# Summing the squares of six RMS norms with a block of ones, in a hybrid decoder step on one core

## The chip, the core and the metric

The kernel runs on one core of a Trainium2 chip. A core has a matrix engine (TensorE, PE in the profile; the loads of its stationary operand stand there as PEld), a vector engine (VectorE, DVE), an activation engine (ScalarE, ACT), a general engine (GpSimd, POOL) and a queue engine that issues the DMAs (SyncE, SP). [...] The metric is the device time of one execution in microseconds (us), as a median over runs.

## The reference, cut to what matters

One decoder layer over 304 tokens (16 meta, 256 prompt, 8 sequences of 4 sample tokens). Every RMS norm divides a token's row by the root of its mean square:

```python
def rmsnorm(x, g):
    xf = x.astype(jnp.float32)
    y = xf * lax.rsqrt(jnp.mean(xf * xf, axis=-1, keepdims=True) + EPS)
    return (y * g.astype(jnp.float32)).astype(x.dtype)

# layer, for prompt and sample tokens
proj = rmsnorm(x, g_mix) @ w_in
lru_out = rmsnorm(hl * gelu(gate_lru), g_lru_out)            # over 2048 features
yg = yg * lax.rsqrt(mean(yg * yg, axis=-1) + EPS)            # SSD: 4 groups of 512 features
x = x + concat([lru_out, yg * g_ssd_out]) @ w_out
x = x + square(relu(rmsnorm(x, g_mlp) @ w_up)) @ w_down
y = rmsnorm(x, g_final)
```

That makes eight norms: one on the input, four on the SSD groups, one on the RG-LRU output, one before the MLP and the last one.

## The kernel before

**Layout.** Features lie on the 128 partitions, tokens on the columns (T = 304 columns, or NT = 288 without the meta tokens). A row of 2048 features is 16 such tiles. The sum over features of one token is therefore a sum over partitions, which only TensorE does here.

**Matrix products.** Weights come from HBM as blocks of 128 output features (1 MB each). `prep` loads a block into one of two buffers `wraw`; ACT copies it, rounded, to `whi`, and DVE subtracts to get `wlo`, in two halves (four buffers of each). The activations are split in the same way into a high and a low part. `gemm` makes 16 x 3 matmuls per block (line 101) into one PSUM bank of a pool of three (`g`); the first three blocks take banks of another pool of five (`s`), from which `bank()` serves all small products too. What follows a block (`post`: read the bank, convolve, gate, square) runs on ACT, DVE and POOL beside the next blocks.

**Order.** Small jobs are Python generators. `pump` advances the first one in the list `gens` at four places in each block, so a `yield` moves what follows it about a quarter of a block (some 12 matmuls) down. A scheduler then lays out each engine's list from the dependences; copies of weights have priority.

**The stages.** (1) Input: the first 13 blocks multiply the x that is not yet normalized (`x0`), and their results are scaled by 1/rms (`rsb`); until `rsb` is there, the posts are kept in the list `held`. `norm_x` makes `rsb`, releases the held posts, and then makes the normalized operands `xa` (line 241 scales, ACT copies `xh`, DVE subtracts `xl`), which the later blocks use. (2) Blocks for the SSD inputs, with the SSD cores of four groups between them; `h` are state tiles, loaded by DMA and split by ACT (`h0h`) and POOL (`h0l`). (3) Blocks for the gates z; `norm_z(g)` norms one group. (4) RG-LRU blocks (`post_gate`, `post_xl`, `gates`). (5) Output projection: 16 blocks on the SSD part, in whose first blocks `norm_lru` runs, and 16 on the LRU part. (6) MLP: four rounds of 16 blocks up and 16 down. (7) The final norm and the store.

**The norm itself.** ACT, DVE or POOL square the tiles and add them up to one tile of 128 partitions. `ms_add` (line 161) then takes this tile as stationary operand, 128 tokens at a time, and a column of ones as moving operand: three products of one column, which put the tokens on the partitions. `rs_from` (lines 163 to 167) takes root and reciprocal of that 128 x 3 tile on ACT and DVE. Two yields later `rs_bcast` (line 169) spreads the result over all partitions again, by three products with the identity (line 172). `norm_x` and `norm_lru` then copy it from PSUM to SBUF on ACT; `norm_z` has DVE read it from PSUM. The norm before the MLP (`norm_x1`) and the last one use `ms_add` and `rs_bcast` too.

Of the kernel before, what the change touches and what calls it, by code (L numbers as in the profile page):

```python
# [8 lines left out]
F32 = mybir.dt.float32  # L9
F32R = mybir.dt.float32r  # L10
AF = mybir.ActivationFunctionType
# [3 lines left out]
P = 128  # L15
T = 304          # 16 meta, 256 prompt, 8 x 4 sample tokens
M0 = 16          # first token whose output is needed
NT = 288         # tokens with an output
FL = 328         # columns of the flat convolution
EXT = 331        # 3 zeros, 272 prompt columns, 8 x (3 old + 4 new) sample columns  # L20
S0 = 275         # first sample column of the flat layout
EPS = 1e-6
NK = 16          # 128-row tiles of a 2048-long contraction

# columns of the per-feature parameters
# [3 lines left out]
# columns of the constants  # L29
# [4 lines left out]
def body(ctx, tc, I, O):  # L34
# [12 lines left out]
    def nm(s):  # L47
        cnt[0] += 1
        return f"{s}_{cnt[0]}"
# [13 lines left out]
    def act(out, in_, f, bias=None, scale=None):  # L63
        kw = {}
        if bias is not None:
            kw["bias"] = bias
        if scale is not None:
            kw["scale"] = scale
        A.activation(out, in_, f, **kw)  # L69
# [3 lines left out]
    # ---------------------------------------------------------------- weights  # L73
# [33 lines left out]
    # blocks: (weights, operands, first column, last column, what follows)  # L107
# [35 lines left out]
    # ---------------------------------------------------------------- constants  # L143
# [14 lines left out]
    # ---------------------------------------------------------------- RMS norm  # L158
# [3 lines left out]

    def rs_from(ms, n):
        r3 = cst.tile([P, 3], F32, tag="r3", bufs=2, name=nm("r3"))
        act(r3[:], ms[:, 0:3], AF.Sqrt, bias=epst[:], scale=1.0 / n)
        V.reciprocal(r3[:], r3[:])
        return r3
# [8 lines left out]
    # ---------------------------------------------------------------- start  # L176
    # The first blocks take x as it comes and their results are scaled by 1 / rms; the
    # normalized x of the later blocks is made meanwhile.
# [40 lines left out]
    def norm_x():  # L219
        for k in range(8, NK):  # L220
            sq = sp.tile([P, EXT], F32, tag="th", bufs=2, name=nm("sq"))
            act(sq[:, :T], xts[k][:], AF.Square)
            tt(V, sqa, sqa, sq[:, :T], ADD)
        for _ in range(7):
            yield
        ms = bank()
        ms_add(ms, sqa, T, True, True)
        r3 = rs_from(ms, 2048.0)
        yield
        yield  # L230
        bc = rs_bcast(r3, T)
        act(rsb[:], bc[:, :T], AF.Copy)
        for b in held:
            b()
        held.clear()
        scaled.append(True)
        yield
        for k in range(NK):
            hi = a1p.tile([P, T], F32R, tag="ah", name=nm("xh"))
            lo = a1p.tile([P, T], F32R, tag="al", name=nm("xl"))  # L240
            tc.keep_in_program_order(V.scalar_tensor_tensor(
                xts[k][:], xts[k][:], par[:, C_GMIX + k:C_GMIX + k + 1], rsb[:], op0=MUL, op1=MUL))
            act(hi[:], xts[k][:], AF.Copy)
            tt(V, lo[:], xts[k][:], hi[:].bitcast(F32), SUB)
            xa.append((hi, lo))
            yield
            yield
            yield
# [3 lines left out]
    # ---------------------------------------------------------------- other resident data  # L252
# [9 lines left out]
    hw = cst.tile([P, 152], F32, name="hw")      # halves of conv_ssd_w, conv_ssd_b; lru_ba, lru_bx  # L262
# [42 lines left out]
    # ---------------------------------------------------------------- SSD: B, C, x  # L305
# [84 lines left out]
    # ---------------------------------------------------------------- SSD core of one group  # L390
# [6 lines left out]
    # Tokens of a chunk on the partitions; "sm" has the 32 sample tokens three times and then the  # L397
    # 16 meta tokens, so that one pass sums the products of high and low parts.
    def ssd_core(g):
# [5 lines left out]
        # C of each sequence in columns of its own, high and low parts  # L405
# [84 lines left out]
        # states: after the meta tokens, after chunk 1, after chunk 2  # L490
        hst = [sq_.tile([P, 512], F32, tag="hst", bufs=3, name=nm("hst")) for _ in range(3)]
        yield
        # decay between the tokens of a chunk, for each head
# [109 lines left out]
    # ---------------------------------------------------------------- input projection, SSD part  # L603
# [33 lines left out]
    def norm_z(g):  # L637
        yield
        yield
        ms = bank()  # L640
        ms_add(ms, yg_sq[g], NT, True, True)
        r3 = rs_from(ms, 512.0)
        yield
        yield
        bc = rs_bcast(r3, NT)
        for i in range(4 * g, 4 * g + 4):
            yy = yt_[i][:, :NT]
            stt(yy, yy, par[:, C_GSSD + i:C_GSSD + i + 1], bc[:, :NT], MUL, MUL)
            if i % 2:
                yield  # L650
# [30 lines left out]
    # ---------------------------------------------------------------- second operand set  # L681
# [14 lines left out]
    # ---------------------------------------------------------------- RG-LRU  # L696
# [80 lines left out]
    # With w = tanh(-log(a) / 2): 1 - a^2 = w (1 + a)^2.  # L777
# [43 lines left out]
    # ---------------------------------------------------------------- output projection  # L821
# [3 lines left out]
    def norm_lru():  # L825
        yield
        yield
        ms = bank()
        ms_add(ms, lsq, NT, True, True)
        r3 = rs_from(ms, 2048.0)  # L830
        yield
        yield
        bc = rs_bcast(r3, NT)
        rs = lp.tile([P, NT], F32, tag="sq", bufs=2, name="rsl")
        act(rs[:], bc[:, :NT], AF.Copy)
        for h in range(16):
            hi = a1p.tile([P, T], F32R, tag="ah", name=nm("lh"))
            lo = a1p.tile([P, T], F32R, tag="al", name=nm("ll"))
            u = us[h][:, :NT]
            stt(u, u, par[:, C_GLRU + h:C_GLRU + h + 1], rs[:], MUL, MUL)  # L840
            act(hi[:, :NT], u, AF.Copy)
            tt(V, lo[:, :NT], u, hi[:, :NT].bitcast(F32), SUB)
            lrua.append((hi, lo))
            yield
# [44 lines left out]
    # ---------------------------------------------------------------- MLP  # L889
    mp = ctx.enter_context(tc.tile_pool(name="mp", bufs=1))  # L890
    # m = mean(x1^2) + eps: x1 + relu(h / sqrt(m))^2 w = (m x1 + relu(h)^2 w) / m; the division
    # goes into the last norm.
# [74 lines left out]
    # ---------------------------------------------------------------- final norm  # L967
# [11 lines left out]
def _tiles(w, m=128):  # L979
    """(2048, n) weights as blocks [n / 128, 128 (row in tile), 16 (tile), 128 (column)]"""  # L980
    n = w.shape[1] // m
    return w.reshape(NK, P, n, m).transpose(2, 1, 0, 3)


def _feat(v):
    """(n,) per-feature values as [128, n / 128]"""
    return v.reshape(-1, P).T
# [79 lines left out]
```

## Time and profile before

| | |
|---|---|
| three runs | 1652.13, 1652.5, 1656.11 us; median 1652.5 |
| profiled execution: span of its instructions | 1649.8 us |
| median of the runs less that span (what lies around it) | 2.7 us |
| mean granted clock of TensorE | 0.995 |
| busy: PE, PEld, DVE, ACT, POOL | 1625.4, 1587.4, 1048.4, 830.7, 248.0 us |

The page gives no time of the profiled execution other than its span. Of PE's idle time 10.2 us lie in the first 20 us and 11.3 us in the last 20 us (by a table of busy time in stretches), where data come in and results go out. A name such as `g` or `whi` is the program's, without its number; "128*128 128x304" is a stationary operand of 128 x 128 and 304 moving columns. Matmuls are pipelined, so the length shown of one is longer than its share of the engine's time: its cost is read from the start of one to the start of the next.

### The profile page before, as it was taken

The page shows a single profiled execution, that of the slowest core. Times are in us where ns is not written, and L with a number is a line of the kernel's source. Part 1 is how long each engine was busy: PE and PEld are TensorE (multiplying, and loading weights), DVE is VectorE, ACT ScalarE, POOL GpSimd, SP SyncE. Part 2 cuts the span into 40 slices and gives each one's busy share as a digit, 9 for nine tenths or more (in the row PEclk, how much of TensorE's full clock was granted, in tenths as well). Part 3 has the DMA queues.
Part 4 walks back from the last instruction along what each step waited for, and adds up shares of the span by engine and source line. Part 5 has one row for each costly group of instructions (what it writes and reads, how often), then busy time and mean ns, then how long its engine had stood idle before and what let it go on. Part 6 is the DMA issues. An engine that isn't in the chain of part 4 may idle for free.

```text
span 1649.8 us, 29019 instructions
## 1 busy us (share of the span) xinstructions
PE 1625.4 (99%) x11915; PEld 1587.4 (96%) x11915; DVE 1048.4 (64%) x1542; ACT 830.7 (50%) x1299; POOL 248.0 (15%) x311
## 2 busy tenths in 40 slices
PE   7999999999999999999999999999999999999997
PEld 6998888889999999999999999999999999999997
DVE  7989898988778787556565433544445555545554
ACT  5546575566777775344444433443334433344442
POOL 3433443431223221001140000000000000000000
PEclk9999999999999999999999999999999999999998
DMA  6444555554444455544545444454545454544442
GB/s 215 156 167 139 187 180 180 175 186 142 164 161 164 163 169 180 190 168 160 172 154 170 162 162 170 160 172 157 176 156 176 155 169 163 169 164 161 171 157 105
DMA packets 53989, 274.29 MB, mean 166 GB/s; under 512 B 5984, under 2 KB 12768, under 8 KB 24544
## 3 DMA queue, kind: packets, MB, share of 16 engines
q1 hardware_dynamic: 53856, 272.44, 48.9%
q8 instruction: 93, 1.52, 0.4%
q14 instruction: 40, 0.33, 0.1%
HBM read 259.99 MB, written 12.42 MB: 165 GB/s over the span
## 4 chain that ended last, share of the span: by engine, by line
PE 98%; DMA 1%; DVE 0%; SPq 0%; ACT 0%; issue 0%; DVEq 0%; ACTq 0%
PE g L101 90%; PE s L101 1%; PE s L439 1%; PE s L764 1%; PE s L562 1%; PE s L560 1%; PE s L501 1%; PE s L437 0%; PE s L510 0%; DMA wraw<-in_win 0%; PE s L161 0%; PE s L449 0%; DVE z L58 0%; PE s L172 0%; PE s L521 0%; PE s L587 0%
## 5 line engine op out<-in xcount | busy, mean ns | idle before, releaser
L58 DVE TENSOR_TENSOR wlo<-wraw,whi 128x1024 fp32r<-128x1024 f32 (+1 forms) x470 | 573.3, 1221 | 443.8 <-ACT whi L69 443.2
L69 ACT ACTIVATE whi<-wraw 128x1024 fp32r<-128x1024 f32 (+1 forms) x470 | 492.4, 1049 | 683.6 <-PE g L101 630.3
L101 PE MATMUL g<-mh,whi 128*128 128x288 f32 x1024 | 303.2, 296 | 0.0
L101 PE MATMUL g<-hh,whi 128*128 128x288 f32 x1024 | 303.0, 296 | 0.0
L101 PE MATMUL g<-hl,whi 128*128 128x288 f32 x1024 | 302.4, 295 | 0.0
L101 PE MATMUL g<-ml,whi 128*128 128x288 f32 x1024 | 302.1, 295 | 0.0
L101 PE MATMUL g<-hh,wlo 128*128 128x288 f32 x1024 | 301.3, 294 | 0.0
L101 PE MATMUL g<-mh,wlo 128*128 128x288 f32 x1024 | 301.1, 294 | 0.0
L101 PE MATMUL g<-xh,whi 128*128 128x288 f32 (+1 forms) x960 | 288.3, 301 | 3.0 <-DVE ext L288 3.0
L101 PE MATMUL g<-xl,whi 128*128 128x288 f32 (+1 forms) x960 | 287.4, 300 | 0.0
L101 PE MATMUL g<-xh,wlo 128*128 128x288 f32 (+1 forms) x960 | 286.8, 299 | 0.0
L101 PEld LDWEIGHTS g<-mh,wlo 128*128 128x128 f32 x1024 | 192.9, 188 | 0.0
L101 PEld LDWEIGHTS g<-hh,wlo 128*128 128x128 f32 x1024 | 192.8, 188 | 0.0
L101 PEld LDWEIGHTS g<-hh,whi 128*128 128x128 f32 x1024 | 192.5, 188 | 0.0
L101 PEld LDWEIGHTS g<-hl,whi 128*128 128x128 f32 x1024 | 192.5, 188 | 0.0
L101 PEld LDWEIGHTS g<-ml,whi 128*128 128x128 f32 x1024 | 192.3, 188 | 0.0
L101 PEld LDWEIGHTS g<-mh,whi 128*128 128x128 f32 x1024 | 191.9, 187 | 0.0
L101 PEld LDWEIGHTS g<-xh,whi 128*128 128x128 f32 x960 | 180.3, 188 | 6.9 <-DVE ext L288 3.2
L101 PEld LDWEIGHTS g<-xl,whi 128*128 128x128 f32 x960 | 180.4, 188 | 3.9 <-issue 1.0
L101 PEld LDWEIGHTS g<-xh,wlo 128*128 128x128 f32 x960 | 180.6, 188 | 2.8 <-issue 0.2
L101 PE MATMUL g<-lh,whi 128*128 128x288 f32 x256 | 75.8, 296 | 0.0
L101 PE MATMUL g<-sh,whi 128*128 128x288 f32 x256 | 75.7, 296 | 0.0
(272 smaller groups left out, 2327.7 us busy)
## 6 DMA issues: line engine op xcount, KB each, us to landing
wraw<-in_win SPq DMA_DIRECT2D x69, 1024.0 KB, 5.0
wraw<-in_wup SPq DMA_DIRECT2D x64, 1024.0 KB, 4.9
wraw<-in_wdn SPq DMA_DIRECT2D x64, 1024.0 KB, 4.9
wraw<-in_wout SPq DMA_DIRECT2D x32, 1024.0 KB, 4.9
h<-in_stssd SPq DMA_DIRECT2D x32, 256.0 KB, 3.0
out_sssd<-h SPq DMA_DIRECT2D x32, 256.0 KB, 3.5
wraw<-in_win SPq DMA_DIRECT2D x12, 256.0 KB, 5.2
big<-in_x SPq DMA_DIRECT2D x16, 152.0 KB, 3.6
```

The lines of the kernel that those rows point to most:

```text
L58: e.tensor_tensor(out, a, b, op=op)
L69: A.activation(out, in_, f, **kw)
L101: TE.matmul(o, a[:, k % 8, :], b[:, c0:c1], start=n == 0, stop=n == 3 * NK - 1)
L439: TE.matmul(po[0:66, :], cm[:, 66 * b:66 * b + 66], a[:], start=b == 0 and n == 0, stop=b == 7 and n == 1)
L501: TE.matmul(pbc[:, 0:NT], selr[:, h:h + 1].to_broadcast([64, P]), acst[:], start=True, stop=True)
L560: TE.matmul(py[64 * q:64 * q + 64, 128 * c:128 * c + 128], xdc[c][:, 64 * j:64 * j + 64], em[c][:, j, :], start=True, stop=True)
L562: TE.matmul(py[:, 256 + 128 * c:384 + 128 * c], hst[c][:, 128 * t:128 * t + 128], C[:, 16 + 128 * c:144 + 128 * c], start=True, stop=True)
L764: TE.matmul(pr[:, :FL], w_[:, m, :], x_[:], start=n == 0, stop=n == 2)
```

## The change

Six of the eight norms (`norm_x`, four `norm_z`, `norm_lru`) get `ms_all`: the stationary operand is one column of ones, broadcast to 128 x 128, and the tile of summed squares is the moving operand, all 288 or 304 columns in one product. Each output partition then has the sums of all tokens. `rs_all` takes root (ACT, out of PSUM) and reciprocal (DVE, in place) on the whole 128 x 288 or 128 x 304 tile, in SBUF: in `rsb` itself, in a new buffer of the pool `big`, or in `rsl`. The two yields between are gone (in `norm_z` and `norm_lru` one stays, behind the reciprocal). The operands are plain 32-bit floats as before. The rest of the diff takes comments out.

```diff
-    def rs_from(ms, n):
-        r3 = cst.tile([P, 3], F32, tag="r3", bufs=2, name=nm("r3"))
-        act(r3[:], ms[:, 0:3], AF.Sqrt, bias=epst[:], scale=1.0 / n)
-        V.reciprocal(r3[:], r3[:])
-        return r3
...
+    def ms_all(sq, width):
+        ms = bank()
+        TE.matmul(ms[:, :width], ones[:].to_broadcast([P, P]), sq[:, :width], start=True, stop=True)
+        return ms
+
+    def rs_all(out, ms, width, n):
+        act(out, ms[:, :width], AF.Sqrt, bias=epst[:], scale=1.0 / n)
+        V.reciprocal(out, out)
...
     def norm_x():
...
-        ms = bank()
-        ms_add(ms, sqa, T, True, True)
-        r3 = rs_from(ms, 2048.0)
-        yield
-        yield
-        bc = rs_bcast(r3, T)
-        act(rsb[:], bc[:, :T], AF.Copy)
+        ms = ms_all(sqa, T)
+        rs_all(rsb[:], ms, T, 2048.0)
...
     def norm_z(g):
         yield
         yield
-        ms = bank()
-        ms_add(ms, yg_sq[g], NT, True, True)
-        r3 = rs_from(ms, 512.0)
-        yield
-        yield
-        bc = rs_bcast(r3, NT)
+        ms = ms_all(yg_sq[g], NT)
+        bc = bigt()
+        rs_all(bc[:, :NT], ms, NT, 512.0)
+        yield
...
     def norm_lru():
         yield
         yield
-        ms = bank()
-        ms_add(ms, lsq, NT, True, True)
-        r3 = rs_from(ms, 2048.0)
-        yield
-        yield
-        bc = rs_bcast(r3, NT)
+        ms = ms_all(lsq, NT)
         rs = lp.tile([P, NT], F32, tag="sq", bufs=2, name="rsl")
-        act(rs[:], bc[:, :NT], AF.Copy)
+        rs_all(rs[:], ms, NT, 2048.0)
+        yield
```

The change moves instructions of all engines, since the scheduler lays them out anew. Three places:

On DVE at the input norm, before. `s_266` is the bank of the first block (dt), `s_356` that of the second, `rsb` the scale of all held posts.

```order
L58 TENSOR_TENSOR wlo_415<-wraw_412,whi_414 128x1024
L166 RECIPROCAL r_79_409<-r_79_409 128x3
L58 TENSOR_TENSOR wlo_419<-wraw_412,whi_418 128x1024
L58 TENSOR_TENSOR big_452<-s_266,rsb 128x304
L58 TENSOR_TENSOR ext_213<-s_356,rsb 128x272
L58 TENSOR_TENSOR ext_213<-s_356,rsb 128x8x4
L340 TENSOR_SCALAR big_452<-big_452,par 128x304
```

The same place now:

```order
L58 TENSOR_TENSOR wlo_428<-wraw_425,whi_427 128x1024
L178 RECIPROCAL rsb<-rsb 128x304
L58 TENSOR_TENSOR big_409<-s_266,rsb 128x304
L58 TENSOR_TENSOR ext_213<-s_356,rsb 128x272
L58 TENSOR_TENSOR ext_213<-s_356,rsb 128x8x4
L339 TENSOR_SCALAR big_409<-big_409,par 128x304
L58 TENSOR_TENSOR wlo_432<-wraw_425,whi_431 128x1024
```

The reciprocal has become a long one, and the first held posts stand ahead of the next split of weights instead of behind it.

On PE at the end of the three blocks that are the first to use the normalized x, before: their banks are `g_1336`, `g_1455` and `g_1597`. The pool has three banks, so `g_1736` takes the bank of `g_1336` again.

```order
L101 MATMUL g_1336<-xl_1316,whi_1158 128x304
L101 MATMUL g_1336<-xh_1315,wlo_1159 128x304
L101 MATMUL g_1455<-xl_1316,whi_1237 128x304
L101 MATMUL g_1455<-xh_1315,wlo_1238 128x304
L101 MATMUL g_1597<-xh_1266,whi_1332 128x304
...
L101 MATMUL g_1597<-xh_1315,wlo_1333 128x304
L101 MATMUL g_1736<-xh_480,whi_1447 128x304
```

The same place now; the four blocks are `g_1328`, `g_1447`, `g_1589` and `g_1728`.

```order
L101 MATMUL g_1328<-xl_1308,whi_1150 128x304
L101 MATMUL g_1328<-xh_1307,wlo_1151 128x304
L101 MATMUL g_1447<-xl_1308,whi_1234 128x304
L101 MATMUL g_1447<-xh_1307,wlo_1235 128x304
L101 MATMUL g_1589<-xl_927,whi_1324 128x304
...
L101 MATMUL g_1589<-xh_1307,wlo_1325 128x304
L101 MATMUL g_1728<-xh_448,whi_1439 128x304
```

Between the last matmul of the first block and the first one that needs its bank stood 2 + 9 matmuls before; now 2 + 23 stand there.

On ACT at the same place, before: `ext_213<-g_1336` is the first half of the read that sets the bank free (DVE's copy of the sample columns, line 288, is the other).

```order
L69 ACTIVATE whi_1447<-wraw_1445 128x1024
L69 ACTIVATE h0h_1624<-h_236_1519 128x512
L69 ACTIVATE h0h_1715<-h_237_1521 128x512
L69 ACTIVATE whi_1451<-wraw_1445 128x1024
L69 ACTIVATE ext_213<-g_1336 128x272
L69 ACTIVATE whi_1589<-wraw_1587 128x1024
L69 ACTIVATE ext_215<-g_1455 128x272
```

The same place now:

```order
L69 ACTIVATE h0h_1616<-h_234_1511 128x512
L69 ACTIVATE h0h_1707<-h_235_1513 128x512
L69 ACTIVATE whi_1439<-wraw_1437 128x1024
L69 ACTIVATE whi_1443<-wraw_1437 128x1024
L69 ACTIVATE ext_213<-g_1328 128x272
L69 ACTIVATE ext_215<-g_1447 128x272
L69 ACTIVATE whi_1581<-wraw_1579 128x1024
```

The two splits of state tiles have moved ahead of both copies of weights (and their four loads on SP ahead of the load of `wraw_1579`), and the two reads of banks stand side by side.

## Rows read from the trace of the kernel before

**Rows 1.** The page, part 1: span; busy us (share) and instructions.
```profile
span 1649.8 us, 29019 instructions
PE 1625.4 (99%) x11915; PEld 1587.4 (96%) x11915; DVE 1048.4 (64%) x1542; ACT 830.7 (50%) x1299; POOL 248.0 (15%) x311
```

**Rows 2.** Busy time in stretches: us, then each engine's busy us (instructions), clock, DMA.
```profile
100.00:175.00 75.00, 72.02 (x491) 67.39 (x490) 67.10 (x125) 45.52 (x97) 28.36 (x47) 1.00 0.45 151
175.00:371.00 196.00, 196.00 (x1331) 165.90 (x1330) 172.56 (x282) 120.83 (x261) 78.69 (x74) 1.00 0.54 181
371.00:404.00 33.00, 33.00 (x263) 32.91 (x261) 27.59 (x71) 22.87 (x41) 5.94 (x8) 1.00 0.43 145
660.00:1630.00 970.00, 970.00 (x7295) 970.00 (x7294) 489.86 (x553) 399.89 (x511) 33.53 (x31) 1.00 0.49 164
```

**Rows 3.** Timeline of PE, input norm: start us, us, what, count, [idle before <-releaser].
```profile
38.11 0.30 PE L101 MATMUL g<-x0h,whi 128*128 128x304 f32 x1
38.25 0.72 PE L161 MATMUL s<-ones,sqx 128*128 128x1 f32 x6
38.83 0.39 PE L101 MATMUL s<-x0h,whi 128*128 128x304 f32 x1
39.05 0.30 PE L101 MATMUL s<-x0l,whi 128*128 128x304 f32 x1
...
42.25 0.76 PE L172 MATMUL s<-con,r 128*128 128x128 f32 x6
42.84 0.38 PE L101 MATMUL s<-x0h,whi 128*128 128x304 f32 x1
```

**Rows 4.** Instructions of lines 510 and 473: ns min/median/max, first and last start.
```profile
L510 PE MATMUL s<-xw,bt x16: 590/592/593, 170.2 to 356.5; 128*128 128x512 f32 x16
...
L473 PE MATMUL s<-cf,bf x8: 275/275/275, 150.0 to 321.0; 128*128 128x128 f32 x8
```

**Rows 5.** Timeline of ACT, input norm.
```profile
39.01 0.26 ACT L69 ACTIVATE r<-s,epst 128x3 f32<-128x3 f32 x1 [0.89 <-PE s L161]
...
43.28 0.41 ACT L69 ACTIVATE rsb<-s 128x304 f32<-128x304 f32 x1
```

**Rows 6.** Timeline of DVE, input norm.
```profile
39.30 0.17 DVE L166 RECIPROCAL r<-r 128x3 f32<-128x3 f32 x1 [1.23 <-ACT r L69]
43.40 1.22 DVE L58 TENSOR_TENSOR wlo<-wraw,whi 128x1024 fp32r<-128x1024 f32 x1 [3.93 <-ACT whi L69]
44.55 0.47 DVE L58 TENSOR_TENSOR big<-s,rsb 128x304 f32<-128x304 f32 x1
```

**Rows 7.** Instructions of line 271: ns min/median/max.
```profile
L271 DVE RECIPROCAL th<-th x1: 2045/2045/2045, 118.4 to 118.4; 128x304 f32<-128x304 f32 x1
```

**Rows 8.** Timeline of PE around 125 us.
```profile
124.15 0.30 PE L101 MATMUL g<-xh,wlo 128*128 128x304 f32 x1
...
125.67 0.30 PE L101 MATMUL g<-xh,wlo 128*128 128x304 f32 x1
128.96 0.41 PE L101 MATMUL g<-xh,whi 128*128 128x304 f32 x1 [2.98 <-DVE ext L288]
```

**Rows 9.** Timeline of ACT at the same place.
```profile
123.88 1.41 ACT L69 ACTIVATE h0h<-h 128x512 fp32r<-128x512 f32 x2 [0.83 <-DMA h<-in_stssd]
125.19 1.04 ACT L69 ACTIVATE whi<-wraw 128x1024 fp32r<-128x1024 f32 x1
126.14 0.38 ACT L69 ACTIVATE ext<-g 128x272 f32<-128x272 f32 x1
```

**Rows 10.** Timeline of DVE at the same place.
```profile
126.27 2.15 DVE L58 TENSOR_TENSOR wlo<-wraw,whi 128x1024 fp32r<-128x1024 f32 x1
...
128.72 0.18 DVE L288 COPY ext<-g 128x32 f32<-128x32 f32 x1
```

**Rows 11.** Timeline of ACT, then of DVE, ahead of the four group norms.
```profile
373.77 1.06 ACT L69 ACTIVATE whi<-wraw 128x1024 fp32r<-128x1024 f32 x1 [1.47 <-PE g L101]
...
374.86 1.23 DVE L58 TENSOR_TENSOR wlo<-wraw,whi 128x1024 fp32r<-128x1024 f32 x1 [2.55 <-ACT whi L69]
```

More of the change, by code (lines that the diff above doesn't have):

```diff
@@ L827, in norm_lru @@
         yield
-        ms = bank()
-        ms_add(ms, lsq, NT, True, True)
-        r3 = rs_from(ms, 2048.0)
+        ms = ms_all(lsq, NT)
+        rs = lp.tile([P, NT], F32, tag="sq", bufs=2, name="rsl")
+        rs_all(rs[:], ms, NT, 2048.0)
         yield
-        yield
-        bc = rs_bcast(r3, NT)
-        rs = lp.tile([P, NT], F32, tag="sq", bufs=2, name="rsl")
-        act(rs[:], bc[:, :NT], AF.Copy)
         for h in range(16):
```

## The prediction, made before the changed kernel was run

> **What bounds the kernel.** I read the busy shares first, then a table of stretches, then PE's waits in its timeline. The page shows PE busy for 1625.4 of 1649.8 us [rows 1]. The stretches show where the rest can be: from 175 to 371, 371 to 404 and 660 to 1630 us PE is busy all the time; from 100 to 175 it lacks 3.0 us [rows 2]. What is idle beyond that lies in the first and last 20 us, which the change does not touch: the first changed instruction runs at 38 us, and the last norm stays. So two things count: how much time of PE the norms take, and the one wait of PE between. That wait stands at 125 us: the matmul at 128.96 is 2.98 us late and the releaser is DVE's copy `ext`, line 288 [rows 8]. It is a wait for a PSUM bank.
>
> **The work on PE.** The three one-column products of an old norm stand as six instructions, since each product of plain floats is two. They begin at 38.25 and the next block goes on at 38.83, so 0.58 us; the first matmul behind them then holds PE for 0.22 instead of 0.14 us (38.83 to 39.05, against 38.11 to 38.25), 0.08 more [rows 3]. The three spreading products take 0.59 us in the same way (42.25 to 42.84) and I give them the same 0.08. A norm takes 0.66 + 0.67 = 1.33 us, six take 8.0.
>
> The new product is not in the trace at this width. Plain-float products with 512 and 128 moving columns show 592 and 275 ns for each instruction [rows 4]: (592 - 275) / 384 = 0.826 ns per column. Two instructions over 304 columns stream for 2 x 304 x 0.826 = 0.50 us, over 288 for 0.48; with 0.08 behind them 0.58 and 0.56. One at 304 and five at 288: 3.4 us. The saving is 8.0 - 3.4 = 4.6 us, all on PE, which has nothing else to wait for. Bounds: without the 0.08 the six cost 2.9 us; if the lengths shown (by the same two rows 0.42 and 0.41 us for each instruction) were to add up, 5.4. So 2.6 to 5.1 saved; I keep 4.6, since the streaming rate rests on the rows nearest in kind.
>
> [...] The six one-column instructions take 0.58 us, 97 ns from start to start [rows 3]. [...]
>
> **The input norm.** Before, root (0.26 us at 39.01) and reciprocal (0.17 at 39.30) were quick, but the spreading product stood two quarters of a block further down PE's list, at 42.25, and the copy to `rsb` at 43.28; DVE idled 3.93 us, and the held posts began at 44.55 [rows 3, 5, 6]. Now ACT's root over 304 columns can start at 39.0; its nearest row is the copy of 304 columns out of PSUM, 0.41 us [rows 5]. The reciprocal of 128x304 has a row: 2.045 us [rows 7]. So `rsb` is ready near 41.5 us, inside the time in which DVE idled. The long reciprocal costs nothing there, and the first held posts are done before the split of weights at 43.40, as the new list has it; DVE is 1 to 2 us ahead from there. If it were not hidden, it would cost at most its 2 us.
>
> **The wait at 125 us.** The first block on the normalized x has its last matmul at 124.15; its bank is free when the matmul at 128.96 goes, 4.8 us later [rows 8]. ACT split two state tiles first (123.88, after a wait for their DMA), then a half of weights, and read the bank at 126.14; DVE came to its part at 128.72, behind a split of weights of 2.15 us [rows 9, 10]. PE had 11 matmuls to fill this and lost 128.96 - 125.67 - 0.14 = 3.15 us. The new list of PE has 25 there: 14 x 0.14 = 1.96 us more. With the same 4.8 us the loss falls to 1.2. On ACT the state tiles now stand ahead of both halves of weights, their loads are issued ahead of a weight load, and DVE is ahead, so the 4.8 may shrink and the whole 3.15 go. Against that, the load of weights now behind the state tiles may come late. Bounds 0 to 3.15 saved; I take 2.0, the part that rests on a count. Late next is then the copy of the following block's bank, which stands right behind.
>
> **The group norms.** Four reciprocals of 128x288, 2.045 x 288 / 304 = 1.94 us each against 0.17, put 7.1 us on DVE, mostly between 371 and 404 us, where it is busy 27.6 of 33 [rows 2]: some 2 us too much, and two of them stand close together in the new list. What waits behind them is the split of weights `wlo` and the posts. The cover: a half of weights is begun when a buffer is free (ACT at 373.77), is finished by DVE at 376.09 [rows 11], and is used three halves later, 3 x 24 x 0.133 = 9.6 us after 373.77 (0.133 is 970 us by 7295 matmuls [rows 2]). That is 7.3 us of lead, and a bank is read with two blocks to spare. I cost this at nothing; without cover it is up to 7.1 us. The sixth norm, on the LRU output, is used only after the rest of the sixteen blocks beside which it runs; cost nothing. ACT gains and loses little: six roots of 0.41 for 0.26, two copies of 0.41 less, and two more table loads in its list, with a third of its time free in that stretch [rows 2].
>
> **Other moves.** From 130 to 404 us the scheduler reorders small products and DVE work. PE shows no wait there [rows 2]; the number of changes between kinds of product stays about the same, apart from those taken out. I take 0, with bounds from 2 us gained (about as much as 25 such changes of 0.08 us) to 5 us lost (two waits of the size seen at 125 us, less one).
>
> **The sum.** 1649.8 - 4.6 - 2.0 = 1643.2 us of span. The page gives no time for that execution beyond its span; the median of the runs is 2.7 us above it, so 1645.9 us.
>
> **The rivals.**
> (1) The wait at 125 us stays or comes back elsewhere at the same price. For it: DVE is busy 67 of 75 us there, and a list that fits one order need not fit another. Against it: 14 more matmuls of cover. Then only PE's own work counts: 1652.5 - 4.6 = 1647.9 us, no change that can be told (a measurement of this kernel tells about 0.3%, 5 us).
> (2) New waits in the reordered stretch take back what PE saves: 4.6 saved, 3 us lost, 1650.9 us. For it speaks that the list there was drawn up anew, against it that before only one such wait was left.
> (3) Slower: the reciprocals make DVE the bound. Place: the four group norms and the input norm. From the point at which DVE falls more than the 7.3 us of lead behind, PE waits for `wlo`, and each added us of DVE is one of PE: 1.9 us for each of six reciprocals, 11.3 us, so 1652.5 - 4.6 + 11.3 = 1659.2 us. For it: DVE is busy 88% from 175 to 371 us. Against it: after 404 us it has room, and the backlog I count is 2 us.
> (4) All goes well: no wait is left at 125 us and DVE's lead saves some changes of product: 1652.5 - 4.6 - 3.15 - 1 = 1643.8 us.
>
> **How the numbers follow.** The forecast has 0.48, rival 4 0.10, rival 1 0.25, rival 2 0.10, rival 3 0.07. Faster by over 0.3% (below 1647.5) are the forecast and rival 4: 0.58. Within 0.3% are rivals 1 and 2: 0.35. Slower is rival 3: 0.07. The range from 1642.5 to 1651.0 takes in the first four cases with the bounds on the new product (2 us worse, 0.5 better), and leaves out rival 3 and the tails.
>
> **What will show it.** In the new profile: PE goes from block to block across the input norm with a gap of about 0.6 us, once; two instructions of 128x304, each near 0.42 us long. DVE's reciprocal at about 39.5 us takes about 2.0 us and the held posts begin before 42 us. The matmul behind the bank at about 125 us waits under 1.5 us. Between 371 and 430 us PE has no wait for `wlo` or for a bank. PE's busy time falls by about 4.6 us. It is wrong if PE's waits between 47 and 620 us add up to more than 3 us, or if the new product holds PE for more than 0.8 us.

## The result and the profile after

| | before | changed |
|---|---|---|
| median of 4 runs | 1652.32 us (1651.52 to 1656.11) | 1643.54 us (1643.02 to 1644.08) |
| ratio | | 0.9943, 95% interval 0.993 to 0.9957 |
| span of the profiled execution | 1649.8 us | 1642.2 us (run 1644.08 us) |

The changed kernel is faster by 8.8 us. The prediction was 6.6 us faster, 1645.9 us, range 1642.5 to 1651.0. On another chip the same kernel gave 1644.08 us where the kernel before gave 1654.0.

First the page, its busy shares, and the table of stretches, both of the changed kernel.

```profile
span 1642.2 us, 28891 instructions
PE 1620.9 (99%) x11855; PEld 1582.3 (96%) x11855; DVE 1057.7 (64%) x1542; ACT 832.5 (51%) x1299; POOL 243.9 (15%) x311
```
```profile
100.00:175.00 75.00, 74.56 (x497) 69.47 (x496) 67.30 (x125) 47.08 (x98) 29.55 (x47) 0.98 0.47 158
175.00:371.00 196.00, 196.00 (x1336) 166.18 (x1335) 171.56 (x286) 118.94 (x260) 65.37 (x72) 1.00 0.52 178
371.00:404.00 33.00, 33.00 (x245) 32.79 (x245) 31.22 (x66) 24.93 (x40) 6.71 (x9) 1.00 0.52 179
```

Against [rows 1, 2], the hole of 3.0 us between 100 and 175 us has shrunk to 0.4, and nothing opened from 175 to 404. DVE has 9 us more to do in all and fills 31.2 instead of 27.6 of the 33 us around the group norms. In the first line the clock column (third from the end) is 0.98 instead of 1.00; more on that below.

The input norm, PE's timeline, answers to [rows 3]:

```profile
36.97 0.30 PE L101 MATMUL g<-x0h,whi 128*128 128x304 f32 x1
37.11 0.68 PE L173 MATMUL s<-sqx,ones 128*128 128x304 f32 x2
37.39 0.53 PE L101 MATMUL s<-x0h,whi 128*128 128x304 f32 x1
37.76 0.30 PE L101 MATMUL s<-x0l,whi 128*128 128x304 f32 x1
```

The two instructions begin 0.14 us after one another like any others, but the matmul behind them holds PE for 0.37 instead of 0.14 us. From 37.11 to 37.76 minus that one matmul's 0.14 is 0.51 us for the whole norm, once. Before it was 0.66 us and, later, 0.67.

ACT, then DVE at the same place, answer to [rows 5, 6]:

```profile
37.82 0.52 ACT L69 ACTIVATE rsb<-s,epst 128x304 f32<-128x304 f32 x1 [0.93 <-PE s L173]
```
```profile
38.37 2.05 DVE L178 RECIPROCAL rsb<-rsb 128x304 f32<-128x304 f32 x1 [1.52 <-ACT rsb L69]
40.46 0.47 DVE L58 TENSOR_TENSOR big<-s,rsb 128x304 f32<-128x304 f32 x1
...
42.11 1.23 DVE L58 TENSOR_TENSOR wlo<-wraw,whi 128x1024 fp32r<-128x1024 f32 x1 [0.45 <-ACT whi L69]
```

The reciprocal runs where DVE idled. The first held post begins at 40.46 instead of 44.55, ahead of the split of weights and not behind it.

The bank wait: PE, ACT, DVE and DMA issues of the changed kernel, answering to [rows 8 to 10].

```profile
120.21 0.30 PE L101 MATMUL g<-xh,wlo 128*128 128x304 f32 x1
...
123.66 0.30 PE L101 MATMUL g<-xh,wlo 128*128 128x304 f32 x1
124.39 0.41 PE L101 MATMUL g<-xh,whi 128*128 128x304 f32 x1 [0.44 <-DVE ext L287]
```
```profile
119.99 2.01 ACT L69 ACTIVATE whi<-wraw 128x1024 fp32r<-128x1024 f32 x2 [3.72 <-PE g L101]
121.91 0.66 ACT L69 ACTIVATE ext<-g 128x272 f32<-128x272 f32 x2
```
```profile
123.02 1.22 DVE L58 TENSOR_TENSOR wlo<-wraw,whi 128x1024 fp32r<-128x1024 f32 x1
124.16 0.28 DVE L287 COPY ext<-g 128x32 f32<-128x32 f32 x2
```
```profile
111.89 1.75 SPq L420 DMA_DIRECT2D h<-in_stssd  x4
115.64 0.33 SPq L78 DMA_DIRECT2D wraw<-in_win  x1
```

PE loses 124.39 - 123.66 - 0.14 = 0.59 us instead of 3.15. Two things helped. More matmuls stand in front: the bank's last one is at 120.21, and the 25 behind it cover 3.45 us (123.66 - 120.21) where 11 covered 1.52 (125.67 - 124.15), so 1.93 us. And the bank comes free 4.18 us after its last matmul, not 4.81, which is 0.63 us: ACT no longer has state tiles `h` in front of it (their loads are issued at 111.89, before the next load of weights at 115.64), and DVE's split takes 1.22 instead of 2.15 us.

The group norms: the products of line 173 and the reciprocals of line 178 (ns min/median/max, first and last start). They answer to [rows 7] and are what [rows 11] were to cover.

```profile
L173 PE MATMUL s<-big,ones x8: 404/406/435, 369.3 to 399.0; 128*128 128x288 f32 x8
```
```profile
L178 DVE RECIPROCAL big<-big x4: 1940/1942/1954, 375.6 to 405.1; 128x288 f32<-128x288 f32 x4
```

PE's list of waits for the changed kernel holds those of the first 20 us and of the end, and between them only the 0.44 us above.

**A ledger.** Count the matmuls of the weight blocks (line 101) in PE's timeline: there are 11184 in every kernel, and the n-th starts earlier or later in one trace than in another. The gain or loss in each stretch is the change of that lead (us; plus is gained). The counts were chosen so that one cause falls into each stretch.

| | to 120 (start) | to 240 (input norm) | to 768 (bank wait) | to 1080 | to 3000 (group norms) | to 4500 (LRU norm) | to 11183 | end | span |
|---|---|---|---|---|---|---|---|---|---|
| before to changed | 1.13 | 0.82 | 2.62 | -1.46 | 3.34 | 0.84 | 0.00 | 0.24 | 7.5 |
| the same, second profiles (the last two experiments) | -0.10 | 0.82 | 2.90 | 2.60 | 3.33 | 0.84 | 0.00 | 0.71 | 11.1 |

The norms give 0.82 + 3.34 + 0.84 = 5.0 us, the wait 2.6. The first and fourth stretch differ between two pairs of executions of the same two kernels, so they are not the change's. Behind the fourth are falls of the granted clock (to 0.51 and 0.52, below) and, in the second profile of before, two short waits for state tiles near 193 us (0.3 and 0.2 us); the first is the start, where the clock (below) and the waits for `x` differ from one execution to the next (PE's waits for `x0h` and `x0l` come to 10.2 and 9.9 us in the first pair, 10.4 and 9.3 in the second). In the first pair these terms nearly cancel (1.13 - 1.46 + 0.24), so that its 7.5 us come close to 5.0 + 2.6 by chance.

### The profile page after: what moved, and what is told of

Its sections match the earlier page's. It is cut to its first block, busy times and chain, and to the rows that moved or that the text cites. A ratio compares the mean times of both kernels' runs of the same rounds, so it can differ in the third digit from the quotient of the medians.

```text
span 1642.2 us, 28891 instructions
## 1 busy us (share of the span) xinstructions
PE 1620.9 (99%) x11855; PEld 1582.3 (96%) x11855; DVE 1057.7 (64%) x1542; ACT 832.5 (51%) x1299; POOL 243.9 (15%) x311
## 3 DMA queue, kind: packets, MB, share of 16 engines
q8 instruction: 93, 1.52, 0.4%
## 4 chain that ended last, share of the span: by engine, by line
PE 98%; DMA 1%; DVE 0%; SPq 0%; issue 0%; ACT 0%; DVEq 0%
PE g L101 90%; PE s L101 1%; PE s L438 1%; PE s L761 1%; PE s L561 1%; PE s L559 1%; PE s L500 1%; PE s L436 0%; PE s L509 0%; DMA wraw<-in_win 0%; PE s L448 0%; DVE z L58 0%; PE s L520 0%; PE s L586 0%; DMA big<-in_x 0%; SPq L209 0%
```

## The experiments

Theory A: the gain is a sum of places, PE's own work in six norms and the bank wait, and the wait went because the posts of the first blocks stand earlier, not because the product is new. Rivals: the new layout as a whole (B), the reciprocals limit (D), others as named. All times are medians; the kernel before was run beside each group of runs.

### One part alone

**Only the input norm** (the kernel before with this edit):

```
-        ms = bank()
-        ms_add(ms, sqa, T, True, True)
-        r3 = rs_from(ms, 2048.0)
-        yield
-        yield
-        bc = rs_bcast(r3, T)
-        act(rsb[:], bc[:, :T], AF.Copy)
+        ms = ms_all(sqa, T)
+        rs_all(rsb[:], ms, T, 2048.0)
```

> The kernel before, with the input norm alone changed. Theory A (the gain is a sum of places: the products that PE no longer runs, and the bank wait): the input norm holds PE 0.5 us once instead of 0.66 + 0.67 us, 0.8 us less; PE's list up to the 18th block is that of the changed kernel, with 25 matmuls instead of 11 ahead of the matmul that wants the bank, so the wait at about 124 us loses about 0.6 instead of 3.15 us. Nothing else changes: 3.4 us less, 1648.9 us, and from 130 us on the two traces run in step until the end. Rival B (the new layout of the lists or the freer ACT bring the gain, wherever the norms are): some 8 us less, near 1644.5 us. Rival C (the bank wait went because of the later norms' layout): the wait stays near 3 us and the time is 1651.5 us.

Measured: 1648.43 us, ratio 0.9966 (0.9954 to 0.9978), span 1646.2. Ledger against before: start -0.02, input norm 0.82, bank wait 2.62, then 0.12 and -0.14, then 0.00 up to the last matmul. By the ledger that is A to the tenth: the input norm alone takes away 2.62 of the 3.15 us of the wait, as the full change does, and B and C fall. The medians differ by more, 5.7 us (1654.14 beside it), since many executions of before are longer than the profiled one; the paragraph "Open" below returns to this.

**Only the four group norms** (the kernel before with this edit in `norm_z`):

```
-        ms = bank()
-        ms_add(ms, yg_sq[g], NT, True, True)
-        r3 = rs_from(ms, 512.0)
-        yield
-        yield
-        bc = rs_bcast(r3, NT)
+        ms = ms_all(yg_sq[g], NT)
+        bc = bigt()
+        rs_all(bc[:, :NT], ms, NT, 512.0)
+        yield
```

> The kernel before, with the four group norms alone changed. Theory A: the wait at 125 us stays at 3 us, since PE's list up to there is that of before; each group norm takes 0.9 us of PE's time less, 3.5 us in all between 370 and 440 us, 1648.8 us; the four reciprocals of 1.94 us make no wait of PE. Rival B (it is the layout): no gain or a loss of a few us, 1652 us. Rival D (the reciprocals are not hidden behind the matmuls): up to 7 us on PE, so 3 us slower, 1656 us.

Measured: 1652.13 us, ratio 0.9987 (0.9978 to 0.9996), span 1650.1. The group norms gave 2.28 us, 1.06 less than in the changed kernel: this list has a wait of 0.59 us of its own, at an LRU product (line 771) for `xch`. D falls, B falls in part (the layout takes back a third). A's time, 1648.8 us, was missed by 3.3 us: besides that 1.06 us, the bank wait, with the list of before, came out longer, 4.08 us, and behind it the granted clock fell to 0.51 (130.3 to 133.7 us), which cost 1.5 us by the ledger. ACT's row and PE's row in this trace:

```profile
124.73 1.27 ACT L69 ACTIVATE h0h<-h 128x512 fp32r<-128x512 f32 x2 [2.19 <-DMA h<-in_stssd]
```
```profile
129.55 0.41 PE L101 MATMUL g<-xh,whi 128*128 128x304 f32 x1 [4.08 <-DVE ext L297]
```

ACT waited 2.19 us for the state tiles, against 0.83 in [rows 9]; PE waited 1.1 us longer. So the wait varies between executions, and goes with how long ACT waits for that load.

### Which feature of the input norm takes the wait away

**Posts late** (the changed kernel):

```
         rs_all(rsb[:], ms, T, 2048.0)
+        yield
+        yield
         for b in held:
```

> The changed kernel, with the held posts of the first blocks begun two quarters of a block later, as the kernel before had them; the norms are all as changed. PE's list then has 10 matmuls between the last one of the first normalized block and the one that wants its bank (25 in the changed kernel, 11 in the one before). Theory A1 (the count of matmuls covers the wait): with the 3.9 us that the bank took in the changed kernel the loss is 3.9 - 9 x 0.14 = 2.6 us, with the 4.8 us of the kernel before 3.4; so 2 to 3 us slower than the changed kernel, near 1646 us. Theory A2 (the bank comes free sooner, since the state tiles and their loads stand earlier; the count matters little): the loss stays under 1 us, 1643.5 us.

Measured: 1648.03 us, ratio 0.9967 (0.9953 to 0.998), span 1645.7.

```profile
123.97 0.63 ACT L69 ACTIVATE h0h<-h 128x512 fp32r<-128x512 f32 x1 [2.17 <-DMA h<-in_stssd]
```
```profile
127.74 0.41 PE L101 MATMUL g<-xh,whi 128*128 128x304 f32 x1 [2.15 <-DVE ext L289]
```

The wait is back with all six new norms in place, 2.31 us lost where A1 said 2.6 (one state tile, not two, stands ahead of the bank on ACT). A2 falls. The 3.9 us in A1 was counted from the last matmul of the second block; from that of the first it is 4.18 us in the changed kernel, which would make 2.9 us, and in this trace 3.85. The time is 2 us above A1's 1646: behind the wait the granted clock fell again, to 0.52 (129.3 to 132.7 us), 1.7 us by the ledger against the second trace of the changed kernel.

**The old input norm, only without its two yields:**

```
         r3 = rs_from(ms, 2048.0)
-        yield
-        yield
         bc = rs_bcast(r3, T)
```

> The kernel before; all norms sum and spread as before, but the input norm's spreading products are put in the list right behind the root, not two quarters of a block later. PE's list then has 24 matmuls ahead of the one that wants the bank at about 125 us, against 11 before and 25 in the changed kernel. Theory A (the wait goes by where the posts of the first blocks stand, not by the new product): the wait loses 0.6 to 1.3 us instead of 3.15, no PE time is saved in the norm, the rest of the trace runs in step with before: 2 to 2.5 us less, 1650 us. Rival G (it is the norm's own shorter chain, with no second product and no copy, that brings the bank sooner): the wait stays at 3 us, 1652.3 us.

Measured: 1649.99 us, ratio 0.9982 (0.9974 to 0.9991), span 1647.7; ledger against before: input norm -0.01, bank wait 2.62, nothing else over 0.3.

```profile
126.60 0.41 PE L101 MATMUL g<-xh,whi 128*128 128x304 f32 x1 [0.42 <-DVE ext L286]
```

The whole gain at 125 us comes from two deleted lines of the old norm. G falls.

**A fourth bank for the blocks** (the kernel before):

```
-    psg = ctx.enter_context(tc.tile_pool(name="psg", bufs=3, space=PSUM))
-    pss = ctx.enter_context(tc.tile_pool(name="pss", bufs=5, space=PSUM))
+    psg = ctx.enter_context(tc.tile_pool(name="psg", bufs=4, space=PSUM))
+    pss = ctx.enter_context(tc.tile_pool(name="pss", bufs=4, space=PSUM))
```

> The kernel before with four banks instead of three for the blocks and four instead of five for all other products; no norm is changed. It tells what the wait at 125 us is worth by itself. Theory A: the wait at the bank is gone and nothing takes its place: 3.1 us less, 1649.2 us. Rival E (DVE and ACT are behind there whatever the bank, so PE waits for the next weights or for another bank instead): the wait comes back in another place within 10 us, 0 to 1 us less, 1652 us. Rival F (the small products need their five banks): new waits between 150 and 400 us, 5 us slower or more.

Measured: 1660.91 us, ratio 1.0041 (1.0025 to 1.0057). At 125 us the wait is gone and the ledger gains 3.15 us there, as A has it; but F decides. PE's waits (us, times, longest), and two stretches of the table:

```profile
PE s L439 <- ACT h0h L69: 2.0, 2, 1.4
...
PE s L437 <- DVE hst L58: 1.0, 1, 1.0
PE s L439 <- POOL h0l L58: 0.9, 1, 0.9
```
```profile
260.00:275.00 15.00, 13.65 (x62) 9.26 (x62) 12.90 (x29) 3.01 (x6) 5.50 (x5) 0.54 0.67 225
...
325.00:333.00 8.00, 7.17 (x32) 5.85 (x33) 5.32 (x13) 2.20 (x5) 4.03 (x4) 0.57 0.62 204
```

In both, PE has small products with pauses between, and the mean granted clock is 0.54 and 0.57: some 10 us lost by it (15 x 0.46 + 8 x 0.43, an estimate from the two rows), besides waits of 5.4 us in all, of which the three largest rows are shown.

### The sizes

**Each product of ones twice** (the changed kernel; the same line once more in `ms_all`):

```
         TE.matmul(ms[:, :width], ones[:].to_broadcast([P, P]), sq[:, :width], start=True, stop=True)
+        TE.matmul(ms[:, :width], ones[:].to_broadcast([P, P]), sq[:, :width], start=True, stop=True)
```

> The changed kernel with each of its six products of ones run twice into the same bank; everything else, the order of the lists included, is the same. It measures the price of the new product. Theory A (the new product takes what the trace of the changed kernel shows from start to start: two instructions at 0.14 us, then a pause of some 0.2 us behind it, which a second product does not bring again): 0.28 us for each of the six more products, 1.7 us slower than the changed kernel. Rival (by the prediction's rate of 0.83 ns per column and instruction plus 0.08 us): 0.56 us each, 3.4 us slower.

Measured: 1646.58 us, ratio 0.9966 (0.9953 to 0.9978). Ledger against the changed kernel: -0.53 at the input norm, -1.98 at the four group norms, -0.48 at the LRU norm, and 0.01 at the bank wait: 2.99 us, 0.50 for each.

```profile
37.55 0.68 PE L173 MATMUL s<-sqx,ones 128*128 128x304 f32 x2
38.07 0.68 PE L174 MATMUL s<-sqx,ones 128*128 128x304 f32 x2
38.35 0.53 PE L101 MATMUL s<-x0h,whi 128*128 128x304 f32 x1
38.72 0.30 PE L101 MATMUL s<-x0l,whi 128*128 128x304 f32 x1
```

My reading of the start times as a price was wrong, and the prediction's rate (0.83 ns for each column and instruction, 0.50 us for 304 columns) right: the second product starts 0.52 us after the first. The pause seen behind a product is the rest of the product.

**Reciprocals of the group norms three times** (the changed kernel):

```
         rs_all(bc[:, :NT], ms, NT, 512.0)
+        V.reciprocal(bc[:, :NT], bc[:, :NT])
+        V.reciprocal(bc[:, :NT], bc[:, :NT])
```

> The changed kernel with the reciprocal of each of the four group norms taken three times in a row (the value stays the same), 8 x 1.94 = 15.5 us more of DVE's time between about 375 and 425 us; up to 365 us the lists are the same. It measures how much cover the reciprocals have. Theory A (hidden: DVE is busy 24.9 of the 33 us from 371 to 404 in the changed kernel, and has a lead of 7 us): the first 8 us go into DVE's idle time, the rest into the lead, so PE waits 0 to 4 us in all. Rival D (DVE is already near its bound there, the lead used up by the four reciprocals): PE waits 8 us or more, each added us of DVE beyond the idle time being one of PE.

Measured: 1646.76 us, ratio 0.9964 (0.9952 to 0.9976); ledger over the group norms and the stretch to matmul 4500: -4.15 + 0.63 = -3.5 us. PE's waits for DVE in this trace, and the stretch behind (of the second row, 0.4 us is the bank wait at 125 us, which is not new):

```profile
PE g L101 <- DVE wlo L58: 1.1, 2, 0.5
...
PE g L101 <- DVE ext L287: 0.9, 3, 0.4
```
```profile
404.00:440.00 36.00, 35.03 (x254) 34.34 (x253) 36.00 (x63) 22.66 (x39) 4.90 (x7) 1.00 0.52 176
```

DVE is busy all 36 of 36 us, and only now PE waits for `wlo` and for banks there, some 1.5 us; the rest of the 3.5 us shows in no wait. 15.5 us more of DVE cost 3.5: some 12 us of cover were left in the changed kernel. D falls. But A's account of the cover was wrong: 24.9 is ACT's figure in that row, and DVE is busy 31.2 of the 33 us, so 1.8 us were idle and not 8. The cover lies further on: from 404 to 440 us DVE was busy 31.7 us in the changed kernel and is now 36.0, from 440 to 480 us 30.6 and now 34.9.

### The two norms that were left, and a version that is faster

**All eight norms in the new way** (the changed kernel; `eb` is eps times the squared mean on all partitions, `ms_sum` the product of `ms_all` into a given bank):

```
-    stt(r3[:], msf[0][:, 0:3], 1.0 / 2048.0, e3[:], MUL, ADD)
-    act(r3[:], r3[:], AF.Sqrt)
-    V.reciprocal(r3[:], r3[:])
-    bc = rs_bcast(r3, NT)
+    stt(bc[:], msf[0][:, :NT], 1.0 / 2048.0, eb[:], MUL, ADD)
+    act(bc[:], bc[:], AF.Sqrt)
+    V.reciprocal(bc[:], bc[:])
...
-        ms_add(ms, lsq, NT, True, True)
-        act(mx3[:], ms[:, 0:3], AF.Identity, bias=epst[:], scale=1.0 / 2048.0)
...
-        bc = rs_bcast(mx3, NT)
-        act(msb[:], bc[:, :NT], AF.Copy)
...
+        ms = ms_all(lsq, NT)
+        act(msb[:], ms[:, :NT], AF.Identity, bias=epst[:], scale=1.0 / 2048.0)
```

> The changed kernel with the last two norms done in the new way too. Theory A: the norm behind the output projection saves PE 0.8 us; the first half of the final norm saves 0.1 us; at the end, where nothing covers DVE, the step from the last product to the first scaling (2.4 us in the changed kernel) loses the spreading product (0.9 us) and gains 0.25 us at the sum, 0.2 at the root and 1.77 at the reciprocal, so about 1.3 us more: in all the same as the changed kernel, within 0.6 us. Rival (a new product is a gain wherever it stands): 1.7 us faster than the changed kernel.

Measured: 1643.93 us, ratio 0.9946 (0.9934 to 0.9958). Ledger against the changed kernel: 0.85 at the norm behind the output projection, 0.18 at the first half of the final norm, -1.34 at the end. A, within 0.1 us. DVE at the end:

```profile
1629.41 0.46 DVE L61 SCALAR_TENSOR_TENSOR rfb<-s,eb 128x288 f32<-128x288 f32 x1 [1.32 <-PE s L891]
1630.37 1.95 DVE L960 RECIPROCAL rfb<-rfb 128x288 f32<-128x288 f32 x1 [0.51 <-ACT rfb L69]
1632.36 0.76 DVE L58 TENSOR_TENSOR z<-z,rfb 128x576 f32<-128x576 f32 x1
```

Here the 1.95 us of the reciprocal stand bare in a chain, where the old form has 0.18 us.

**Seven norms** (the changed kernel; the norm behind the output projection as in the kernel above; the final norm in the old way, its small term put into the sum beforehand):

```
-                    V.tensor_copy(lsq[:], sq[:])
+                    tt(V, lsq[:], eb[:], sq[:], ADD)
...
-    stt(r3[:], msf[0][:, 0:3], 1.0 / 2048.0, e3[:], MUL, ADD)
-    act(r3[:], r3[:], AF.Sqrt)
+    act(r3[:], msf[0][:, 0:3], AF.Sqrt, scale=1.0 / 2048.0)
```

> The changed kernel with the norm behind the output projection done in the new way too, the final norm as before. The final norm's small term (eps times the squared mean) is put into the sum of squares beforehand, so that at the end the root reads the bank at once and one DVE step goes. Theory A (a new product is worth 0.85 us wherever PE is the bound and something covers DVE; the end is a chain without cover): PE 0.85 us less at about 817 us, and 0.2 to 0.4 us less between the last product and the first scaling (2.4 us in the changed kernel): 1.1 us faster than the changed kernel, 1642.5 us. Rival (the end is bound by the stores): 0.85 us faster.

Measured: 1642.45 us, ratio 0.9937 (0.9925 to 0.995), the fastest here; the changed kernel on the same chip 1644.08. That difference is less than a measurement tells, but the ledger has the 0.85 us. The end, in this execution, took 0.38 us longer:

```profile
1629.68 0.83 PE L161 MATMUL s<-ones,sr 128*128 128x1 f32 x6 [1.02 <-ACT sr L69]
1630.98 1.49 PE L166 MATMUL s<-con,rf 128*128 128x128 f32 x6 [0.47 <-DVE rf L956]
```

From sum to spreading product it is 1.30 us (1.53 in the changed kernel), so the step removed is seen; but the spreading products took 1.49 instead of 0.85 us, at a granted clock of 0.50. What the end gives at full clock was not seen.

### The same kernels once more

The kernel before, unchanged:

> The kernel before, unchanged, for a second profile of it. Theory A (the wait at 125 us hangs on a load of state tiles that ACT waits for, and so varies between executions; the granted clock falls to half now and then, at the start and after 125 us, whatever the norms are): the bank wait is between 2.5 and 4.5 us, longer than 3.0 us if ACT waits for the tiles longer than 0.83 us, and shorter if it waits less; between 20 and 27 us and perhaps between 125 and 150 us the clock is halved for 0 to 8 us. Rival: the wait and the clock are the same in each execution of one kernel: 3.0 us, and half clock from 18 to 26 us alone.

Measured: 1654.4 us, ratio 1.0001; 12 executions from 1651.52 to 1657.53. ACT waited 1.35 us for the state tiles, and PE 3.25 us for the bank, between [rows 8] and the trace of the group norms alone. Then:

```profile
128.50:129.20 0.70, 0.70 (x5) 0.70 (x6) 0.70 (x1) 0.11 (x1) 0.70 (x1) 1.00 1.13 152
129.20:132.70 3.50, 3.50 (x16) 3.50 (x15) 3.41 (x8) 0.00 (x0) 2.44 (x4) 0.52 0.87 300
```

Less than a us after the wait the granted clock falls to 0.52 for 3.5 us, which costs 1.56 us by the ledger.

The changed kernel, unchanged:

> The changed kernel, unchanged, for a second profile of it on the chip on which the kernel before runs. Theory A: the bank wait is 0.4 us again, since ACT waits for no load there; the half clock from 146 to 150 us need not come back, and where it does not, PE is 1.6 us earlier behind it. Time 1643 to 1644 us. Rival (the fall of the clock at 146 us belongs to the new order): it comes back at the same matmul.

Measured: 1644.08 us, ratio 0.9945 (0.9932 to 0.9958); 1642.97 to 1644.33. The bank wait is 0.43 us again. The fall of the clock at 146 us, which the first trace of the changed kernel has, is not there; one line of each, first trace and second:

```profile
146.00:149.00 3.00, 3.00 (x15) 2.97 (x14) 2.94 (x8) 0.10 (x1) 2.08 (x6) 0.51 0.00 0
```
```profile
146.00:149.00 3.00, 3.00 (x23) 2.58 (x22) 2.94 (x8) 0.71 (x3) 2.08 (x6) 1.00 0.01 3
```

The rival falls: the list is the same and the clock is not.

## Why the prediction was right, and where its sizes were off

1. **PE's work.** Forecast 4.6 us (8.0 out, 3.4 in), measured 5.0 by the ledger, 0.82 to 0.85 for a norm. The new product costs 0.50 (doubled) instead of the 0.56 to 0.58 taken; so an old norm cost about 0.84 + 0.50 = 1.34 us, where the sum had 1.33. The step that was a little off is the 0.08 us added behind the new product.
2. **The bank wait.** Forecast 2.0 saved, measured 2.56 to 2.6. The part that was priced is right: 14 more matmuls were to cover 1.96 us and covered 1.93. The term is short by the part that was left out: the 4.8 us until the bank is free was kept, and fell to 4.2, 0.63 us more. That it could was said; it was not put into the sum. The cause given holds: late posts bring the wait back, early ones with the old norm remove it.
3. **The input norm's reciprocal.** Forecast hidden, from about 39.5 us for 2.0 us, posts before 42 us. It ran 38.37 to 40.42, the post at 40.46; DVE's idle time took it.
4. **The group norms' reciprocals.** Forecast hidden behind 7.3 us of lead. Nothing of it shows on PE; three times the reciprocals showed that the cover is larger, some 12 us beyond what the change uses, and that much of it is idle time of DVE behind 404 us, which the prediction did not count.
5. **Other moves.** Forecast 0 (-2 to 5 lost). With the full change it is 0 within 0.2 us, once the clock is taken out. With the group norms alone a new layout cost 1.06 us, so the doubt was a fair one.
6. **The sum.** 5.0 + 2.6 is 1.0 us more than the 6.6 forecast. The other 1.3 or 1.4 us between 1645.9 and 1643.5 are not the change's: the time beyond the span was taken as 2.7 us, as median less span, but is 1.9 in the changed kernel's run and 1.7 to 2.3 in the others; and this profiled execution was 0.5 us above the median of its own kernel. Rival 4 (all goes well) came nearest, 1643.8, by luck: it had 4.6 + 3.15 from norms and wait, close to the 7.6 measured, but also 1 us from fewer changes of product, which did not show, and the same 2.7 us beyond the span.

PE's busy time fell by 4.5 us, as the prediction wanted to see. That is weak evidence: stretches at a lower clock, different in the two traces, lengthen busy time too (from 146 to 149 us PE is busy 3.00 of 3.00 us in both traces of the changed kernel, with 15 matmuls at 0.51 and 23 at 1.00).

Open: whether the wait brings the fall of the clock behind it. In the four traces with a wait of over 2 us at the bank the clock fell within 2 us behind it in three (after waits of 4.08, 3.25 and 2.15 us, to 0.51, 0.52 and 0.52) and not in one (2.98; 1.00 from 129 to 134 us); in the eight with 0.44 us or less in none there, though in two at 146 or 147 us (to 0.51 in the first trace of the changed kernel), behind a run of small products. Each of these falls cost some 1.6 us by the ledger. Times on record speak for a link. The old input norm without its two yields takes the wait away and keeps the norms of before: its 12 executions lie within 0.8 us (1649.7 to 1650.5, mean granted clock 0.995 or 0.996), where the 17 of before beside them spread over 5.8 us (1651.2 to 1657.0, clock 0.992 to 0.998). With the group norms alone, where the wait stays, 12 executions spread over 5.3 us, again at 0.992 to 0.998. If it is so, removing the wait is worth more than 2.6 us in the longer executions, and part of the 8.8 us between the medians is that: the lowest times of the two kernels differ by 8.5 us, the profiled spans by 7.5. One fall does not make a spread of 5.8 us, and no execution of before above 1654.0 us was profiled, so where those lose their time is not shown.

## What to carry to other kernels

Price a change on the bottleneck engine by what it displaces from start to start, and check it by doing it twice: the shown length (0.42 us an instruction) and the start interval (0.14) both mislead, the doubled product (0.50 for two instructions) does not. Ask what a shorter chain lets run earlier: a third of this gain came from posts that two yields had held back, 85 us upstream of the wait, and could be had without the new product. Trading PE time for DVE time pays where DVE has cover (six norms, a seventh too), and gives it back where the chain is bare, as at the end (1.34 us).

## What the runs showed of the hardware

- **The clock.** One list of instructions ran at different granted clocks: behind the bank wait 0.52 for 3.5 us in one trace of before and 1.00 in the other; from 146 to 149 us 0.51 in one trace of the changed kernel and 1.00 in the other. Close ahead of three falls PE had waited at the bank (4.08, 3.25 and 2.15 us); ahead of the one at 146 us it was busy all of 142 to 146 (4.00 of 4.00 us). What brings the falls is not shown.
- **The clock at the start.** By single us, the clock column shows 0.50 to 0.82 from 18 to 26 us in one trace of before, 0.50 to 0.75 from 20 to 24 in the other, 0.50 to 0.92 from 19 to 24 in the first of the changed kernel, and 1.00 throughout in the second. There the column is not enough: in that second trace the matmuls begin 0.25 us apart until 24 us, and 0.14 apart from then on, so PE ran at little more than half its later pace at the start there too.

```profile
22.42 0.46 PE L101 MATMUL s<-x0l,whi 128*128 128x304 f32 x1
22.68 0.46 PE L101 MATMUL s<-x0h,wlo 128*128 128x304 f32 x1
...
25.03 0.30 PE L101 MATMUL s<-x0l,whi 128*128 128x304 f32 x1
25.17 0.30 PE L101 MATMUL s<-x0h,wlo 128*128 128x304 f32 x1
```

- **DVE beside POOL.** While POOL subtracted the low parts of two state tiles, from 115.46 to 118.24 us, two instructions of DVE took 1.57 and 1.56 us. The changed kernel, POOL and then DVE:

```profile
115.46 2.78 POOL L58 TENSOR_TENSOR h0l<-h,h0h 128x512 fp32r<-128x512 f32 x2 [3.29 <-ACT h0h L69]
```
```profile
115.53 1.57 DVE L58 TENSOR_TENSOR xl<-big,xh 128x304 fp32r<-128x304 f32 x1
117.02 1.56 DVE L58 TENSOR_TENSOR th<-big,th 128x304 f32<-128x304 f32 x1
```

The same subtraction takes 0.46 to 0.47 us for each of the fifteen other tiles of `xl`, and the instruction on `th` took 0.47 in the kernel before, with POOL idle. The 2.15 us of `wlo` in [rows 10], which begin at 126.27, against a median of 1.225 over the whole trace, fit this: in the kernel before POOL's work stood there.

```profile
124.59 2.75 POOL L58 TENSOR_TENSOR h0l<-h,h0h 128x512 fp32r<-128x512 f32 x2 [9.75 <-PE g L101]
```

In the changed kernel POOL's work stands ahead, and the split on the way to the bank takes 1.22 us. No run moves POOL's work alone, so that it slowed DVE is not shown.
